# A two-layer decoder trunk in split fp32: matmul widths in runs of four, wide projections for the short convolution, the decays' clamp on ACT

## The chip, the cores and the metric

The kernel runs on one core of a Trainium2 chip. A core has five engines with a queue each: PE (TensorE, the matmuls; PEld is its loading of the stationary operand), DVE (VectorE), ACT (ScalarE), POOL (GpSimd) and SP (SyncE, which here issues loads). Each works its queue in order and waits at an instruction until what that one needs is there. Matmuls write PSUM, which has eight banks of 128 x 512 fp32 numbers; the other data is in SBUF, and weights come from HBM by DMA.

The metric is the device time of one execution in microseconds (us). Three runs of the kernel before gave 1529.78 (median), 1529.49 and 1533.1 us.

## The reference

256 tokens of width 1024 pass two layers. In each: a SwiGLU FFN (width 2816), a mixer, a second FFN, and a gated embedding; every step is normed first and added to the stream `h`.

```python
def swiglu(x, wg, wu, wd):
    return (jax.nn.silu(x @ wg) * (x @ wu)) @ wd

def hybrid_mixer(u, w_in, ...):
    proj = u @ w_in
    sc_b, sc_c, sc_x, m_z, m_xbc, m_dt, gate_a, gate_m = jnp.split(proj, PROJ_SPLITS, axis=-1)
    y_a = (sc_b * causal_depthwise_conv(sc_c * sc_x, sc_conv_w)) @ sc_w_out
    xbc = jax.nn.silu(causal_depthwise_conv(m_xbc, m_conv_w) + m_conv_b)
    xs, bm, cm = jnp.split(xbc, ...)
    ...
    y = ssd_chunked(xh * dt[..., None], A * dt, bm, cm)
    ...
    merged = jax.nn.sigmoid(gate_a) * y_a + jax.nn.sigmoid(gate_m) * y_m
    return merged @ w_o
```

In `ssd_chunked` the sequence is cut into two chunks of 128 tokens. Inside a chunk the weight of token s for token l is `exp(a_cum[l] - a_cum[s])` for s <= l and zero otherwise, times a product of the group's `C` and `B`; there are 32 heads in 4 groups of 8.

## The kernel before

**Split products.** Every matmul operand is held as two numbers: `hi`, a rounded copy, and `lo`, the rest. A product is hi x hi + hi x lo + lo x hi. Weights come as raw fp32 by SP's DMAs (`fetch`, 512 KB each); `half` lets ACT write `whi` (L98) and DVE `wlo` (L96). A chunk of weights is two such halves of four k-blocks each (k runs over the 1024 inputs in eight blocks of 128). Up to five raw and seven split halves are alive (`NRAW`, `NHALF`); a new split starts when TensorE has used an old one up.

**Two forms of a projection.** Both have 128 weight columns standing and the 256 tokens moving, with the tokens' hi and lo parts side by side in `both` (512 columns). `ws` (L213) issues three matmuls of 256 columns for each k: `wh` with hi, `wh` with lo, `wl` with hi, all into one half of a bank; two calls (`ws2`) make a chunk of 256 output columns, 48 matmuls, one bank. `wide_ws` (L232) issues two for each k: `wh` with all 512 columns of `both`, so that hi and lo results land in the two halves of a bank, and `wl` with 256 columns into the first half. A bank takes 16 matmuls; what is in its halves has to be added afterwards. Gate and up products in the FFN use it (`up`, L402, two banks a step, 18 steps in each of four FFNs) and `both_parts` (L387) joins the halves with an ACT copy and a DVE add. The mixer's projections use `ws2`.

**The mixer.** `ORDER` lists the large steps of a layer: `bc` and `xs` (projections with the long convolution), `sc` (the short convolution's three projections for each of four groups: g.0 gives `xsb`, g.1 is multiplied with it and convolved in `sc_conv`, g.2 gates it in `sc_gate`), `z`, `ga`, `gm`, `so`. `LAGS` puts the small steps of each SSD group so many large steps behind it. `turn` transposes `xsil` (a convolved `xs`) on TensorE, and ACT copies it to `xg`; `weigh` makes `xw` from `xg` on DVE, and `states` multiplies it on TensorE. `decay` (L960) loads the rows of `a_cum` into `m` by a DMA on ACT's queue, subtracts each token's own `acum` and clamps at 0 on DVE (L968, eight heads one by one), takes `Exp` on ACT and multiplies with the group's `cbm`. `outputs` queues the products of `m` and `xd`, and `drip` slips them in between the matmuls of a later projection. The order within each engine's queue is then set by the framework's scheduler.

**The code around the change.**

Of the kernel before, what the change touches and what calls it, by code (L numbers as in the profile page):

```python
# [8 lines left out]
F32 = mybir.dt.float32  # L9
F32R = mybir.dt.float32r  # L10
BF16 = mybir.dt.bfloat16
AF = mybir.ActivationFunctionType
ALU = mybir.AluOpType
# [3 lines left out]
P = 128  # L17
# [5 lines left out]
KD = D // P  # L23
# [12 lines left out]
NT2 = 8  # L36
# [23 lines left out]
def trunk(ctx: ExitStack, tc: tile.TileContext, a: dict, out: bass.AP):  # L60
    nc = tc.nc
# [10 lines left out]
    def nm(s):  # L72
        cnt[0] += 1
        return f"{s}_{cnt[0]}"

    def bank():
        return psp.tile([P, 512], F32, tag="ps", name=nm("ps"))

    def mm(o, l, r, start, stop):
        return nc.tensor.matmul(o, lhsT=l, rhs=r, start=start, stop=stop).ins  # L80
# [55 lines left out]
    def chunk(name, i, c, kn):  # L136

        key = (name, i, c)
        sources[key] = (a[name][i, c], kn)
        return key  # L140
# [52 lines left out]
    def xpair():  # L193

        both = act.tile([P, KD, 2, NT, P], F32R, tag="xx", name=nm("xx"), bufs=2)
        return both[:, :, 0], both[:, :, 1], both.rearrange("p k s t c -> p k (s t c)")
# [11 lines left out]
    def drip(n=1):  # L208
        for _ in range(min(n, len(fill))):
            fill.pop(0)()  # L210


    def ws(o, wc, cols, x, t=None):  # L213
        xh, xl, _ = x
        for k in range(KD):
            wh, wl = wc[k]
            rh = xh[:, k] if t is None else xh[:, k, t]
            rl = xl[:, k] if t is None else xl[:, k, t]
            mm(o, wh[:, cols], rh, k == 0, False)
            mm(o, wh[:, cols], rl, False, False)  # L220
            mm(o, wl[:, cols], rh, False, k == KD - 1)
            drip()

    def ws2(ps, wc, x, t=None):

        for b in range(2):
            o = ps[:, b * 256:(b + 1) * 256] if t is None else ps[:, b * 256 + t * P:b * 256 + (t + 1) * P]
            ws(o, wc, slice(b * P, (b + 1) * P), x, t)

    def wide_ws(o, wc, cols, x):  # L232
        xh, _, both = x
        for k in range(KD):
            wh, wl = wc[k]
            if k < KD - 1:
                mm(o, wh[:, cols], both[:, k], k == 0, False)
                mm(o[:, 0:256], wl[:, cols], xh[:, k], False, False)
            else:
                mm(o[:, 0:256], wl[:, cols], xh[:, k], False, False)  # L240
                mm(o, wh[:, cols], both[:, k], False, True)


    def as_(os, lh, ll, rh, rl, first, last):
# [135 lines left out]
    class FFN:  # L380
        def __init__(self, i, gu, dn, gname, ple=None):
# [20 lines left out]
            def up(j):  # L402
                def f(wc):
                    banks[j] = [bank(), bank()]
                    for b in range(2):
                        wide_ws(banks[j][b], wc, slice(b * P, (b + 1) * P), prep.x)
                    evac(j)
                return f, [chunk(gu, i, j, KD)]
# [187 lines left out]
    class Mixer:  # L596
        def __init__(self, i):
# [3 lines left out]
            S = self  # L601
# [6 lines left out]
            def step(fn, *keys):  # L608
                add_.append((fn, keys))
# [38 lines left out]

            def sc_step(g, n):
                def f(wc):  # L650
                    ps = bank()
                    ws2(ps, wc, S.prep.x)
                    if n == 0:
                        if g == 0:
                            S.sct = xpair()
                        S.xsb[g] = mp.tile([P, 512], F32, tag="t2", name=nm("xsb"), bufs=NT2)
                        nc.scalar.activation(S.xsb[g], ps, AF.Copy)
                    elif n == 1:
                        S.sc_conv(g, ps)
                    else:  # L660
                        S.sc_gate(g, ps)
                step(f, chunk("w_sc", i, g * 3 + n, KD))

            def z_run(g, kh, ts):
# [175 lines left out]
        def t2(self, what, shape=(P, GW)):  # L840
            return self.pool.tile(list(shape), F32, tag="t2", name=nm(what), bufs=NT2)

        def conv_silu(self, ps, blk, dst):

            ac = self.t2("ac", (P, 2, 256))
            for b in range(2):
                q = blk + b
                src = ps[:, b * 256:(b + 1) * 256]
                nc.scalar.activation(ac[:, b], src, AF.Identity, scale=self.convw[:, q, 3:4], bias=self.convb[:, q:q + 1])  # L849
                for s in range(1, 4):  # L850
                    nc.vector.scalar_tensor_tensor(ac[:, b, s:256], src[:, 0:256 - s], self.convw[:, q, 3 - s:4 - s],  # L851
                                                   ac[:, b, s:256], op0=ALU.mult, op1=ALU.add)
            nc.scalar.activation(dst, ac, AF.Silu)
# [106 lines left out]
        def decay(self, g, c):  # L960
            mp = self.pool
            cbm = mp.tile([P, P], F32, tag="cbm", name=nm("cbm"), bufs=2)
            nc.vector.tensor_tensor(cbm, self.cps[g][:, c * P:(c + 1) * P], upper, op=ALU.mult)
            self.ms[g, c] = m = mp.tile([P, HG, P], F32, tag="m", name=nm("m"), bufs=2)
            r0 = c * HEADS + g * HG
            nc.scalar.dma_start(m, self.acD[r0:r0 + HG, :].rearrange("(o h) l -> o h l", o=1).partition_broadcast(P))
            for hh in range(HG):
                nc.vector.tensor_scalar(m[:, hh], m[:, hh], self.acum[:, r0 + hh:r0 + hh + 1], 0.0, op0=ALU.subtract, op1=ALU.min)  # L968
            nc.scalar.activation(m, m, AF.Exp)
            nc.vector.tensor_tensor(m, m, cbm.unsqueeze(1).broadcast_to([P, HG, P]), op=ALU.mult)  # L970

        def weigh(self, g):
# [180 lines left out]
```

## Time and profile before

| | |
|---|---|
| runs | 1529.49, 1529.78, 1533.1 us |
| profiled execution, its time | 1528.8 us |
| its span, first to last instruction | 1527.0 us |
| mean granted TensorE clock | 0.999 |
| FFN 1 of layer 0, gate and up products, then down | from 16 to 188 us of the span |
| mixer of layer 0 | about 205 to 541 us |
| FFN 2 of layer 0, then the embedding | 556 to 758 us |
| layer 1, the same three | from 774, 960 and 1311 us |

The page lists each engine's busy time, its share in 40 slices of the span, the chain of work that ended last, and groups of like instructions. A group's row reads: line, engine, operation, what it writes <- what it reads, sizes, count | busy us, mean ns of one | idle time of the engine just before, and what ended it. In a timeline row the first two numbers are the start in us from the span's start and the time taken; TensorE's matmuls overlap their neighbours, so that their cost in a stream is the distance from one start to the next.

### The profile page before, as it was taken

The page shows a single profiled execution, that of the slowest core. Times are in us where ns is not written, and L with a number is a line of the kernel's source. Part 1 is how long each engine was busy: PE and PEld are TensorE (multiplying, and loading weights), DVE is VectorE, ACT ScalarE, POOL GpSimd, SP SyncE. Part 2 cuts the span into 40 slices and gives each one's busy share as a digit, 9 for nine tenths or more (in the row PEclk, how much of TensorE's full clock was granted, in tenths as well). Part 3 has the DMA queues.
Part 4 walks back from the last instruction along what each step waited for, and adds up shares of the span by engine and source line. Part 5 has one row for each costly group of instructions (what it writes and reads, how often), then busy time and mean ns, then how long its engine had stood idle before and what let it go on. Part 6 is the DMA issues. An engine that isn't in the chain of part 4 may idle for free.

```text
span 1527.0 us, 22369 instructions
## 1 busy us (share of the span) xinstructions
PE 1512.6 (99%) x8561; PEld 1313.0 (86%) x8561; DVE 1039.5 (68%) x1543; ACT 880.6 (58%) x1254; POOL 24.7 (2%) x41
## 2 busy tenths in 40 slices
PE   9999999999999999999999999999999999999998
PEld 6888889999988878888878888899999888888886
DVE  6666468898865577664677655688979655766545
ACT  6665366667564366653656654675666544666544
POOL 0000000000000000000000000000000000000000
PEclk9999999999999999999999999999999999999999
DMA  7655566555546555556565555665555555655542
GB/s 275 207 193 183 176 207 198 187 184 180 185 155 197 192 196 191 182 191 193 170 216 180 182 191 167 205 205 186 191 178 176 166 192 182 217 187 186 189 157 90
DMA packets 85437, 285.68 MB, mean 187 GB/s; under 512 B 10577, under 2 KB 10961, under 8 KB 85330
## 3 DMA queue, kind: packets, MB, share of 16 engines
q1 hardware_dynamic: 77968, 267.94, 53.9%
q10 hardware_dynamic: 7362, 16.31, 3.1%
q8 instruction: 67, 1.10, 0.3%
q14 instruction: 40, 0.33, 0.1%
HBM read 283.10 MB, written 1.11 MB: 186 GB/s over the span
## 4 chain that ended last, share of the span: by engine, by line
PE 94%; DVE 3%; issue 1%; ACT 1%; POOL 0%; POOLq 0%; ACTq 0%; DVEq 0%
PE ps L80 92%; DVE wlo L96 2%; PE ps L273 1%; DVE xn L329 1%; PE ps L636 0%; POOL rstd L289 0%; ACT junk L321 0%; DVE xx L277 0%; PE ps L435 0%; ACT whi L98 0%; DVE h L534 0%; DVE h L1030 0%; DVE sg L589 0%; DVE var L283 0%; DVE h L590 0%
## 5 line engine op out<-in xcount | busy, mean ns | idle before, releaser
L96 DVE TENSOR_TENSOR wlo<-raw,whi 128x1024 fp32r<-128x1024 f32 x508 | 616.6, 1223 | 356.3 <-ACT whi L98 345.6
L98 ACT ACTIVATE whi<-raw 128x1024 fp32r<-128x1024 f32 x508 | 534.2, 1058 | 332.9 <-PE ps L80 302.6
L80 PE MATMUL ps<-xx,whi 128*128 128x256 f32 (+1 forms) x2688 | 685.8, 336 | 0.0
L80 PE MATMUL ps<-xx,wlo 128*128 128x256 f32 x1920 | 517.1, 282 | 0.0
L80 PEld LDWEIGHTS ps<-xx,whi 128*128 128x128 f32 x2688 | 446.9, 190 | 44.6 <-issue 4.3
L80 PEld LDWEIGHTS ps<-xx,wlo 128*128 128x128 f32 x1920 | 364.7, 190 | 13.4
L80 PE MATMUL ps<-whi,xx 128*128 128x512 f32 (+1 forms) x1168 | 367.7, 392 | 2.3 <-ACT whi L98 1.4
L80 PEld LDWEIGHTS ps<-whi,xx 128*128 128x128 f32 x1168 | 218.0, 188 | 47.7 <-ACT whi L98 2.7
L80 PE MATMUL ps<-wlo,xx 128*128 128x512 f32 (+1 forms) x584 | 222.8, 388 | 0.6 <-DVE wlo L96 0.6
L80 PE MATMUL ps<-whi,hh 128*128 128x512 f32 x352 | 137.3, 390 | 0.0
L80 PE MATMUL ps<-wlo,hh 128*128 128x512 f32 x352 | 136.9, 389 | 0.0
L80 PEld LDWEIGHTS ps<-wlo,xx 128*128 128x128 f32 x584 | 109.9, 188 | 23.1 <-DVE wlo L96 2.2
L80 PE MATMUL ps<-whi,hl 128*128 128x512 f32 x352 | 113.6, 389 | 0.0
L80 PEld LDWEIGHTS ps<-whi,hl 128*128 128x128 f32 x352 | 66.1, 188 | 13.8
L80 PEld LDWEIGHTS ps<-wlo,hh 128*128 128x128 f32 x352 | 66.1, 188 | 13.6
L80 PEld LDWEIGHTS ps<-whi,hh 128*128 128x128 f32 x352 | 66.1, 188 | 13.4
L851 DVE SCALAR_TENSOR_TENSOR ac<-ps,convw,ac 128x255 f32<-128x255 f32 (+1 forms) x144 | 67.9, 477 | 9.5 <-ACT ac L849 8.1
L389 ACT ACTIVATE sg<-ps 128x256 f32<-128x256 f32 x72 | 27.7, 384 | 64.5 <-PE ps L80 64.5
L80 PE MATMUL ps<-whi,yh 128*128 128x512 f32 x128 | 50.0, 390 | 0.0
L80 PE MATMUL ps<-wlo,yh 128*128 128x512 f32 x128 | 49.8, 389 | 0.0
L396 ACT ACTIVATE sg<-sg 128x256 f32<-128x256 f32 x72 | 30.0, 417 | 33.3 <-DVE sg L390 33.3
L389 ACT ACTIVATE pr<-ps 128x256 f32<-128x256 f32 x72 | 27.7, 385 | 36.9 <-PE ps L80 36.9
(153 smaller groups left out, 1087.8 us busy)
## 6 DMA issues: line engine op xcount, KB each, us to landing
raw<-in_gu SPq DMA_DIRECT2D x176, 512.0 KB, 3.8
raw<-in_dn SPq DMA_DIRECT2D x88, 512.0 KB, 3.6
raw<-in_w_xbc SPq DMA_DIRECT2D x48, 512.0 KB, 4.1
raw<-in_w_sc SPq DMA_DIRECT2D x48, 512.0 KB, 4.1
raw<-in_w_z SPq DMA_DIRECT2D x32, 512.0 KB, 3.9
raw<-in_w_mo SPq DMA_DIRECT2D x32, 512.0 KB, 3.9
raw<-in_w_ga SPq DMA_DIRECT2D x16, 512.0 KB, 4.3
m<-acD ACTq DMA_DIRECT2D x16, 512.0 KB, 4.9
```

What stands on the lines that cost most here:

```text
L80: return nc.tensor.matmul(o, lhsT=l, rhs=r, start=start, stop=stop).ins
L96: return nc.vector.tensor_tensor(lo, src, hi.bitcast(F32), op=ALU.subtract).ins
L98: up = nc.scalar.activation(hi, src, AF.Copy).ins
L273: nc.tensor.transpose(tp[:, j * P:(j + 1) * P], src[:, c:c + P], ident)
L329: ins = nc.vector.scalar_tensor_tensor(xn[:, sl], h[t][:, sl], r, g, op0=ALU.mult, op1=ALU.mult)
L389: nc.scalar.activation(v, ps[:, 256:512], AF.Copy)
L396: nc.scalar.activation(gate, gate, AF.Silu)
L851: nc.vector.scalar_tensor_tensor(ac[:, b, s:256], src[:, 0:256 - s], self.convw[:, q, 3 - s:4 - s], ac[:, b, s:256], op0=ALU.mult, op1=ALU ...
```

## The change

There are three edits. `wide_ws` follows a list, `FOURS`, of (k, part) pairs: two wide matmuls, four narrow, four wide, four narrow, two wide; with the next bank's first two that makes runs of four. It now drips as well. The short convolution's steps call a new `wide`, which takes two banks, joins their halves into one tile `v` of the pool `t2` (eight buffers), and hands `v` to `sc_conv` and `sc_gate` in place of the PSUM bank. In `decay` ACT takes `Relu(acum - m)`, head by head, with a pointer bias, in place of DVE's subtract and min, and `Exp` gets scale -1.

```diff
+    FOURS = [(k, s) for s, ks in enumerate((range(2), range(4), range(2, 6), range(4, 8), range(6, 8))) for k in ks for s in (s % 2,)]
+
     def wide_ws(o, wc, cols, x):
         xh, _, both = x
-        for k in range(KD):
-            wh, wl = wc[k]
-            if k < KD - 1:
-                mm(o, wh[:, cols], both[:, k], k == 0, False)
-                mm(o[:, 0:256], wl[:, cols], xh[:, k], False, False)
+        for n, (k, s) in enumerate(FOURS):
+            if n == KD + 2:
+                drip(KD // 2)
+            if s == 0:
+                mm(o, wc[k][0][:, cols], both[:, k], k == 0, k == KD - 1)
             else:
-                mm(o[:, 0:256], wl[:, cols], xh[:, k], False, False)
-                mm(o, wh[:, cols], both[:, k], False, True)
+                mm(o[:, 0:256], wc[k][1][:, cols], xh[:, k], False, False)
+        drip(KD // 2)
...
             def sc_step(g, n):
                 def f(wc):
-                    ps = bank()
-                    ws2(ps, wc, S.prep.x)
+                    v = S.wide(wc, "xsb" if n == 0 else "scv")
                     if n == 0:
                         if g == 0:
                             S.sct = xpair()
-                        S.xsb[g] = mp.tile([P, 512], F32, tag="t2", name=nm("xsb"), bufs=NT2)
-                        nc.scalar.activation(S.xsb[g], ps, AF.Copy)
+                        S.xsb[g] = v
                     elif n == 1:
-                        S.sc_conv(g, ps)
+                        S.sc_conv(g, v)
                     else:
-                        S.sc_gate(g, ps)
+                        S.sc_gate(g, v)
...
+        def wide(self, wc, what):
+
+            pss = [bank(), bank()]
+            for b in range(2):
+                wide_ws(pss[b], wc, slice(b * P, (b + 1) * P), self.prep.x)
+            v = self.t2(what)
+            for b in range(2):
+                o = v[:, b * 256:(b + 1) * 256]
+                nc.scalar.activation(o, pss[b][:, 256:512], AF.Copy)
+                nc.vector.tensor_tensor(o, o, pss[b][:, 0:256], op=ALU.add)
+            return v
...
             for hh in range(HG):
-                nc.vector.tensor_scalar(m[:, hh], m[:, hh], self.acum[:, r0 + hh:r0 + hh + 1], 0.0, op0=ALU.subtract, op1=ALU.min)
-            nc.scalar.activation(m, m, AF.Exp)
+                nc.scalar.activation(m[:, hh], m[:, hh], AF.Relu, scale=-1.0, bias=self.acum[:, r0 + hh:r0 + hh + 1])
+            nc.scalar.activation(m, m, AF.Exp, scale=-1.0)
```

Instructions in the queues: the orders of SP and POOL stay as they were; ACT and DVE have the same order as before in the FFNs and another one in the mixers. ACT's table loads go from 47 to 51.

On TensorE, the first gate bank of the first FFN (`ps_83_374`; `whi_59_302` and `whi_62_308` are the hi parts of its weights' two halves, `wlo_60_303` and `wlo_63_309` the lo parts, `xx` the tokens). Before:

```order
L80 MATMUL ps_83_374<-xx_7_112,whi_59_302 128x512
L80 MATMUL ps_83_374<-xx_7_112,wlo_60_303 128x256
L80 MATMUL ps_83_374<-xx_7_112,whi_59_302 128x512
L80 MATMUL ps_83_374<-xx_7_112,wlo_60_303 128x256
L80 MATMUL ps_83_374<-xx_7_112,whi_59_302 128x512
L80 MATMUL ps_83_374<-xx_7_112,wlo_60_303 128x256
L80 MATMUL ps_83_374<-xx_7_112,whi_59_302 128x512
L80 MATMUL ps_83_374<-xx_7_112,wlo_60_303 128x256
```

After the change, the whole bank:

```order
L80 MATMUL ps_83_374<-xx_7_112,whi_59_302 128x512 x2
L80 MATMUL ps_83_374<-xx_7_112,wlo_60_303 128x256 x4
L80 MATMUL ps_83_374<-xx_7_112,whi_59_302 128x512 x2
L80 MATMUL ps_83_374<-xx_7_112,whi_62_308 128x512 x2
L80 MATMUL ps_83_374<-xx_7_112,wlo_63_309 128x256 x4
L80 MATMUL ps_83_374<-xx_7_112,whi_62_308 128x512 x2
```

The matmuls are the same sixteen; their order is now two wide, four narrow, four wide, four narrow, two wide, and the last use of each half of the weights is where it was.

On ACT, the first mixer, where SSD group 0's `xsil` is transposed and copied to `xg` (`m_530` and `m_541` before, `m_536` and `m_549` after, are the group's decays of chunk 0 and 1; `xsb` and `sca` belong to the short convolution's group 1). Before:

```order
L969 ACTIVATE m_541_2797<-m_541_2797 128x1024
L853 ACT_TABLE_LOAD
L853 ACTIVATE xsil_511_2614<-ac_512_2615 128x512
L657 ACTIVATE xsb_520_2686<-ps_519_2637 128x512
L98 ACTIVATE whi_534_2779<-raw_533_2777 128x1024
L98 ACTIVATE whi_537_2785<-raw_536_2783 128x1024
L637 ACTIVATE xg_471_2320<-ps_539_2789 128x2x256
L862 ACTIVATE sca_532_2770<-xsb_520_2686,scw_402_1901 128x256 x2
L637 ACTIVATE xg_471_2320<-ps_542_2809 128x2x256
```

After:

```order
L984 ACTIVATE m_536_2664<-m_536_2664 128x1024
L867 ACT_TABLE_LOAD
L867 ACTIVATE xsil_516_2582<-ac_517_2583 128x512
L853 ACTIVATE xsb_526_2639<-ps_524_2605 128x256
L853 ACTIVATE xsb_526_2639<-ps_525_2606 128x256
L853 ACTIVATE scv_539_2710<-ps_537_2676 128x256
L853 ACTIVATE scv_539_2710<-ps_538_2677 128x256
L98 ACTIVATE whi_542_2725<-raw_541_2723 128x1024
L98 ACTIVATE whi_545_2731<-raw_544_2729 128x1024
L876 ACTIVATE sca_540_2716<-xsb_526_2639,scw_402_1901 128x256 x2
L641 ACTIVATE xg_472_2308<-ps_547_2735 128x2x256
L983 ACTIVATE m_549_2743<-m_549_2743,acum_494_2399 128x128 x8
```

The second copy to `xg` and then the `Exp` of `m_549` follow these rows. Four copies out of PSUM stand where one did, and chunk 1's eight relus have come between the two copies to `xg`; the `Exp` of chunk 1, which stood ahead of `xsil`, now stands behind them. In the second layer the order at this place is the same.

## The prediction

> **What bounds the kernel now.** I read the page's parts 1, 2 and 4 first: who is busy, at what clock, and which engine the last-ending chain runs through.
>
> ```profile
> PE 1512.6 (99%) x8561; PEld 1313.0 (86%) x8561; DVE 1039.5 (68%) x1543; ACT 880.6 (58%) x1254; POOL 24.7 (2%) x41
> PEclk9999999999999999999999999999999999999999
> PE 94%; DVE 3%; issue 1%; ACT 1%; POOL 0%; POOLq 0%; ACTq 0%; DVEq 0%
> L98 ACT ACTIVATE whi<-raw 128x1024 fp32r<-128x1024 f32 x508 | 534.2, 1058 | 332.9 <-PE ps L80 302.6 <-issue 16.6 <-DMA raw<-in_gu 6.8
> ```
>
> TensorE is busy in every slice at the full granted clock, and 94% of the chain runs through it. The last row says who waits for whom: ACT, which prepares the weights, sits idle 302.6 us until TensorE hands a weight buffer back, and only 6.8 us for a load. So weights come ahead of need, and time is won only by shortening what stands in TensorE's own queue; it is lost when a product has to wait for an operand. Next, busy time by engine in the stretch of gate and up products and in the mixer's dense stretch:
>
> ```profile
> core 0: us, PE busy (x) PEld busy (x) DVE busy (x) ACT busy (x) POOL busy (x), PEclk, DMA share, GB/s
> 41.35:131.50 90.15, 90.15 (x514) 78.37 (x513) 62.43 (x100) 56.88 (x99) 0.00 (x0) 1.00 0.58 191
> 229.00:397.00 168.00, 168.00 (x1296) 160.80 (x1295) 144.33 (x272) 110.60 (x147) 2.85 (x4) 1.00 0.56 186
> ```
>
> In both TensorE has no gap. In the first DVE and ACT are 69% and 63% busy; in the second DVE is 86% busy and ACT 66%.
>
> **Widths in runs, gate and up.** The start-to-start time of matmuls is what a chain of them costs. Two rows of the chain view (start, length, matmuls) give it for long runs of one width, 48 of 256 columns and 252 of 512:
>
> ```profile
> 271.10 5.75 PE ps L80 x48
> 464.06 57.16 PE ps L80 x252
> ```
>
> That is 0.1198 and 0.2268 us each. The timeline (start, time, tile, count) shows one gate or up bank of 16 matmuls, today alternating, from one bank's last wide matmul to the next bank's:
>
> ```profile
> 60.70 0.63 PE L80 MATMUL ps<-xx,whi 128*128 128x512 f32 x2
> 61.17 0.28 PE L80 MATMUL ps<-xx,wlo 128*128 128x256 f32 x1
> ...
> 63.28 0.40 PE L80 MATMUL ps<-xx,wlo 128*128 128x256 f32 x2
> 63.52 0.63 PE L80 MATMUL ps<-xx,whi 128*128 128x512 f32 x2
> ```
>
> A bank takes 63.52 - 60.70 = 2.82 us. At the long-run pitches its eight wide and eight narrow matmuls would take 8 x 0.2268 + 8 x 0.1198 = 2.773, so the fourteen changes of width cost 0.047 together. The change keeps four of them. What a run of only four costs is read where widths change once; first wide to narrow, then narrow to wide:
>
> ```profile
> 34.91 0.28 PE L80 MATMUL ps<-xx,wlo 128*128 128x256 f32 x1
> 35.02 0.40 PE L80 MATMUL ps<-xx,whi 128*128 128x512 f32 x1
> ...
> 359.27 0.40 PE L80 MATMUL ps<-whi,xx 128*128 128x512 f32 x1
> 359.50 0.40 PE L80 MATMUL ps<-wlo,xx 128*128 128x512 f32 x1
> 359.74 0.62 PE L80 MATMUL ps<-whi,xx 128*128 128x512 f32 x2
> 360.20 0.39 PE L80 MATMUL ps<-wlo,xx 128*128 128x512 f32 x1
> ```
>
> The first narrow one after a wide run takes 0.11, and the first four wide ones after a narrow run 360.20 - 359.27 = 0.93 instead of 0.907: a wide run pays some settling. Four narrow are 0.11 + 3 x 0.12 = 0.47, four wide 0.93; two of each make 2.80. There are 18 steps x 2 banks x 4 FFNs = 144 banks, so I take 144 x 0.02 = **2.9 us saved**. The best case is no settling, 144 x 0.047 = 6.8. The worst is the two wide matmuls at 60.70, 61.17 - 60.70 = 0.47 or 0.235 each, for all wide ones: 8 x 0.235 + 8 x 0.12 = 2.84, 2.9 us lost. I take the settling rows because they are the nearest to runs of four. TensorE is gapless there, so all of it counts.
>
> [...]
>
> **The short convolution's projections.** There are 24 chunks (12 a layer). Each goes from 48 narrow matmuls, 5.75 us by the row above, to two banks of the new form, 2 x 2.80 = 5.60: 24 x 0.15 = **3.6 us saved** (5.55 and 4.9 at best, 5.68 and 1.7 at worst). TensorE's stretch 229 to 397 is gapless too, so this counts in full. The small products that are dripped between the matmuls come in fours instead of singly; they are as many as before, and I cost that at nothing.
>
> What comes in for it, with the price of each:
>
> ```profile
> L389 ACT ACTIVATE pr<-ps 128x256 f32<-128x256 f32 x72 | 27.7, 385 | 36.9 <-PE ps L80 36.9
> L390 DVE TENSOR_TENSOR sg<-sg,ps 128x256 f32<-128x256 f32 x72 | 30.4, 422 | 17.8 <-ACT sg L389 17.8
> L968 DVE TENSOR_SCALAR m<-m,acum 128x128 f32<-128x128 f32 x128 | 28.8, 281 | 0.0
> L862 ACT ACTIVATE sca<-xsb,scw 128x256 f32<-128x256 f32 x16 | 7.2, 498 | 0.9 <-DVE xsb L857 0.9
> L98 ACT ACTIVATE hh<-pr 128x256 fp32r<-128x256 f32 x72 | 30.2, 419 | 14.7 <-DVE pr L397 14.7
> L853 ACT ACT_TABLE_LOAD x12 | 15.4, 1283 | 0.2
> m<-acD ACTq DMA_DIRECT2D x16, 512.0 KB, 4.9
> ```
>
> A chunk's two halves are joined by two copies on ACT (0.385 each) and two adds on DVE (0.422): 9.2 and 10.1 us a layer. The decays' 64 clamps a layer leave DVE (64 x 0.281 = 18 us). So DVE, the busier of the two, gets lighter.
>
> **The clamp as relu.** No row has 128x128 on ACT with a pointer bias. From 1024 to 256 columns ACT goes from 1.058 to 0.419 us, 0.83 ns a column, so L862 (256 columns, one pointer) less 128 columns is 0.39 us; the bounds are 0.31 (the 419 row less 128 columns, no pointer) and 0.50 (L862 whole). Two of L862 in a row take 0.90 (row at 278.21 below), so each that follows another costs 0.1 less: eight relus take 0.39 + 7 x 0.30 = 2.5 us, and 64 a layer some 20. With two more table loads (2.6) and the copies ACT gains about 30 us a layer, in a stretch where it now is idle 34%. The weights' splits hide that. The DMA that brings `m` was waited for by DVE, and is now waited for by ACT; 4.9 us pass from issue to landing, and behind the first relu stand a table load, `bc`, `xx` and weight splits. Weights are far ahead; I cost that wait at nothing. SP's and POOL's orders stay as they are; the eight DMAs of `m` a layer stay on ACT's queue.
>
> [...]
>
> One place where ACT has the later work is group 0's `xw`. Rows of the timeline now:
>
> ```profile
> 274.81 0.63 ACT L853 ACTIVATE xsil<-ac 128x512 f32<-128x512 f32 x1
> 275.35 0.58 ACT L657 ACTIVATE xsb<-ps 128x512 f32<-128x512 f32 x1
> 275.83 2.01 ACT L98 ACTIVATE whi<-raw 128x1024 fp32r<-128x1024 f32 x2
> 276.69 1.04 PE L636 MATMUL ps<-ident,xsil 128*128 128x128 f32 x8
> 278.21 0.90 ACT L862 ACTIVATE sca<-xsb,scw 128x256 f32<-128x256 f32 x2
> 279.01 0.58 ACT L637 ACTIVATE xg<-ps 128x512 f32<-128x512 f32 x1
> 281.47 0.69 DVE L974 TENSOR_TENSOR xw<-xg,w 128x512 f32<-128x512 f32 x1
> 283.31 1.02 PE L80 MATMUL ps<-xw,btok 128*128 128x512 f32 x2
> ```
>
> `xw` ends at 282.16, 1.15 before TensorE takes it. In the new order ACT does, from the end of `xsil` at 275.44: four copies (4 x 0.29), two splits (2.0), `sca` (0.9), `xg` (0.5), eight relus (2.5) and the second `xg` (0.57), in sum 7.6, so `xg` is there at 283.1 and `xw` at 283.8. What stands ahead of `xsil` comes out even: eight relus (2.5) more, one `Exp` and one table load (2.3) less. TensorE, with five shorter chunks behind it and one more ahead (0.15 each), wants `xw` 0.7 to 0.9 earlier than now, about 282.5. That is **1.3 us of waiting**, in each of two layers: 2.6 us. The bounds are 0 (relus of 0.31) and 2.4 a layer (relus of 0.50, pitch 0.40 or more). After that wait every later operand has that much more time, so I add none further on.
>
> **Sum.** 2.9 + 3.6 - 2.6 = 3.9 us off the profiled execution's 1528.8 gives 1524.9. The median of the runs, 1529.78, lies 1.0 above it, so I name **1525.9 us**. A measurement of this kernel tells about 0.3%, 4.6 us, from no change; the forecast, by itself 1523.3 to 1528.5, lies mostly within that.
>
> **Rivals.** One: the runs settle less and ACT keeps up. Long-run pitches give 6.8 + 4.9 = 11.7, 1518.1; my own gains with no wait give 1523.3. For it: the constant 0.2268 over 252 matmuls; against it the settling rows. Two: the order of widths is worth nothing. A bank stays at 2.82, a chunk becomes 5.64, 24 x 0.11 = 2.6, and the wait takes it back: 1529.8. For it: the wide pair at 0.235 each in today's stream. Three, slower: ACT becomes the late engine in the mixer. The relus stand ahead of both `xsil` and the second `xg`; with waits for `m` in the queue (up to 4.9 where too little stands between its DMA and its relu), TensorE waits there. From 3.3 us a layer the gain of 6.5 is gone, from 5.5 it is slower by over 0.3%; with 6 a layer it is 1535. For it: margins of about a microsecond where ACT gets 30 us more; against: ACT's 34% of idle time and DVE's relief. That the matmuls might not come in fours is no rival: the order shows them so.
>
> **Chances.** Forecast 0.40 (0.12 of it below 1525.2, beyond 0.3%), rival one 0.30, two 0.18, three 0.12. So faster 0.12 + 0.30 = 0.42, same 0.28 + 0.18 = 0.46, slower 0.12. The range takes in rival one to its end and the unknown costs but for all at their worst at once (2.9 lost, 1.7 gained, 4.8 waited: 1535.8), which lies with rival three: 1518 to 1533.5, and leaves out little more than 0.1.
>
> **What would show it.** A gate or up bank of 2.80 us (2.77: rival one; 2.82: two), a projection chunk of 5.60 instead of 5.75; relus near 0.39; TensorE idle before `xw` of group 0 by about 1.3 us with DVE's `xw` as the releaser, and nowhere else in the mixer. Idle time before `xsil`'s transposes, or several microseconds before `xw`, would mean that I costed ACT too low.

## The result, and the profile after

Four runs of the changed kernel gave 1542.45 to 1544.51 us, median 1544.12; the runs of the kernel before beside them had a median of 1531.44. The ratio is 1.0083, with an interval of 1.0070 to 1.0096: **slower by 0.8%**, above the predicted range, where a gain was forecast. The times of the kernel before lie on two levels, about 1529.5 and 1533.3, and the traces show a like step ahead of everything that was changed (the first FFN's long run of products starts at 41 to 42 us in ten of the profiled executions, at 45 in five), while two single runs far above, of 3883 and 2411 us in the first experiment, are in no ratio. The profiled execution has a span of 1540.3 us, 13.3 more than before, and a mean granted clock of 0.995.

The page's busy times and its chain by engine and by line, after the change:

```profile
PE 1513.8 (98%) x8177; PEld 1295.2 (84%) x8177; DVE 1030.1 (67%) x1463; ACT 933.6 (61%) x1426; POOL 24.3 (2%) x41
PE 88%; DVE 5%; ACT 3%; issue 2%; DMA 1%; POOL 0%; POOLq 0%; ACTq 0%; DVEq 0%
```

TensorE's products should take some 6 us less (6.5 by the prediction) and yet it is busy 1.2 us longer, which already says that some ran slowly; its share of the chain went from 94% to 88%. What took its place is in the view of waits of TensorE (what waits, for whom, us in total, times, longest); these three of its rows are new:

```profile
PE ps L640 <- ACT xsil L867: 7.4, 4, 3.7
PE ps L80 <- DVE xw L989: 3.2, 2, 1.6
...
PE ps L277 <- DVE y L1036: 1.1, 2, 0.5
```

Where the time sits in the program, from the chain view: the start of the first mixer's projections and the long run of 252 matmuls near its end, first for the kernel before (whose run of 252 the prediction quotes), then for the changed one, whose FFN stretch stands in front:

```profile
41.35 147.58 PE ps L80 x772
204.85 23.97 PE ps L80 x136
```

```profile
41.70 147.14 PE ps L80 x772
204.74 23.98 PE ps L80 x136
471.10 57.16 PE ps L80 x252
```

The FFN's gate and up piece got 0.44 us shorter. The mixer took 464.06 + 57.16 - 204.85 = 316.37 us and now takes 471.10 + 57.16 - 204.74 = 323.52: 7.15 more, in the second layer 6.95. The place is ACT's queue before the transposes of group 1's `xsil`. ACT and TensorE there after the change, from the timeline (start, time, engine, line; in brackets the idle time before it and what ended it):

```profile
292.02 0.55 ACT L863 ACTIVATE ac<-ps,convb,convw 128x256 f32<-128x256 f32 x1
296.58 0.33 ACTq L980 DMA_DIRECT2D m<-acD  x1
296.96 0.57 ACT L863 ACTIVATE ac<-ps,convb,convw 128x256 f32<-128x256 f32 x1 [4.39 <-PE ps L80]
297.96 1.06 ACT L98 ACTIVATE whi<-raw 128x1024 fp32r<-128x1024 f32 x1 [0.43 <-PE ps L80]
299.40 1.06 ACT L98 ACTIVATE whi<-raw 128x1024 fp32r<-128x1024 f32 x1 [0.38 <-PE ps L80]
300.99 1.28 ACT L983 ACTIVATE m<-m,acum 128x128 f32<-128x128 f32 x4 [0.54 <-DMA m<-acD]
302.29 1.28 ACT L867 ACT_TABLE_LOAD   x1
303.58 0.63 ACT L867 ACTIVATE xsil<-ac 128x512 f32<-128x512 f32 x1
```

```profile
299.82 1.39 PE L80 MATMUL ps<-xd,m 128*128 128x64 f32 x11
304.26 1.12 PE L640 MATMUL ps<-ident,xsil 128*128 128x128 f32 x4 [3.05 <-ACT xsil L867]
```

Read it from the top. The load of the next `m` stands in ACT's queue between the two `ac`, and its issue waits until TensorE has used up an older `m` (there are two buffers). The second `ac` waits behind it, 4.39 us; at most the last 1.5 of these are the issue's doing, since DVE works on the first `ac` until 295.46. Four relus of that new `m` stand ahead of `xsil` and wait for the landing at 300.97. Then come a table load and `xsil`, while TensorE has been idle since 301.21. In the chain it reads as one string, the load from 296.58 to 300.97 and then ACT's own work. The first three rows are group 0's: the load of its first block, from which the chain runs through ACT's queue to `xsil`, and the eight relus of its second block ahead of its `xg`, behind which TensorE waited for `xw`:

```profile
255.68 5.56 DMA m<-acD
...
275.70 0.63 ACT xsil L867
...
280.59 2.33 ACT m L983 x8
...
296.58 4.38 DMA m<-acD
...
301.30 0.97 ACT m L983 x3
...
302.29 1.28 ACT L867
...
303.58 0.64 ACT xsil L867
```

The wait has a second price. The view of windows (stretch, its length, busy time of each engine, then the granted clock) around the wait for `xw`, behind the wait for `xsil`, and behind that of the second layer:

```profile
282.60:284.30 1.70, 0.06 (x2) 0.06 (x1) 0.89 (x3) 1.68 (x4) 0.00 (x0) 1.00 0.27 72
302.65:309.47 6.82, 5.21 (x17) 4.53 (x18) 6.19 (x14) 5.71 (x14) 0.55 (x1) 0.50 0.51 163
309.47:314.00 4.53, 4.53 (x21) 3.74 (x21) 1.40 (x3) 1.93 (x2) 0.00 (x0) 1.00 0.01 3
1067.23:1070.65 3.42, 3.42 (x13) 3.05 (x13) 3.14 (x7) 2.88 (x10) 0.00 (x0) 0.50 0.17 40
```

TensorE worked 5.21 and 3.42 us at half clock. There the 512-column products began 0.427 us apart (six, from 306.67 to 309.23 us), behind it 0.226 (fifteen, from 310.05 to 313.44). From these I put the cost at half of each stretch: 2.6 and 1.7. Before, the clock reads 0.50 only from 1524 us on, when TensorE has no more products.

### The profile page after: what moved, and what is told of

The parts are those of the page before. It is cut to its first block, busy times and chain, and to the rows that moved or that the text cites. A ratio compares the mean times of both kernels' runs of the same rounds, so it can differ in the third digit from the quotient of the medians.

```text
span 1540.3 us, 21647 instructions
## 1 busy us (share of the span) xinstructions
PE 1513.8 (98%) x8177; PEld 1295.2 (84%) x8177; DVE 1030.1 (67%) x1463; ACT 933.6 (61%) x1426; POOL 24.3 (2%) x41
## 4 chain that ended last, share of the span: by engine, by line
PE 88%; DVE 5%; ACT 3%; issue 2%; DMA 1%; POOL 0%; POOLq 0%; ACTq 0%; DVEq 0%
PE ps L80 86%; DVE wlo L96 2%; PE ps L277 1%; DMA m<-acD 1%; ACT whi L98 1%; ACT m L983 1%; DVE xn L333 1%; PE ps L640 0%; ACT L867 0%; POOL rstd L293 0%; DVE xx L281 0%; ACT xsil L867 0%; ACT junk L325 0%; PE ps L439 0%; DVE h L538 0%
## 5 line engine op out<-in xcount | busy, mean ns | idle before, releaser
L80 PE MATMUL ps<-xx,whi 128*128 128x512 f32 (+1 forms) x2304 | 571.6, 361 | 0.0
L80 PEld LDWEIGHTS ps<-xx,whi 128*128 128x128 f32 x2304 | 381.1, 190 | 38.1 <-issue 4.3
L80 PE MATMUL ps<-xx,wlo 128*128 128x256 f32 x1920 | 353.0, 281 | 0.0
L80 PEld LDWEIGHTS ps<-xx,wlo 128*128 128x128 f32 x1920 | 309.0, 189 | 32.4
L293 POOL TENSOR_TENSOR rstd<-var,mhalf 128x1 f32<-128x1 f32 x34 | 23.4, 691 | 1511.1 <-DVE var L287 999.5
```

Of the source, the lines that this page charges most:

```text
L293: nc.gpsimd.tensor_tensor(r, v, mhalf, op=ALU.pow)
```

## The experiments

**The parts, one by one.** First theory: the relus are late on ACT. Rivals: the joins of the wide short convolution are, or the new order of widths costs TensorE itself something.

The clamp back on DVE, the rest as changed:

```diff
-                nc.scalar.activation(m[:, hh], m[:, hh], AF.Relu, scale=-1.0, bias=self.acum[:, r0 + hh:r0 + hh + 1])
-            nc.scalar.activation(m, m, AF.Exp, scale=-1.0)
+                nc.vector.tensor_scalar(m[:, hh], m[:, hh], self.acum[:, r0 + hh:r0 + hh + 1], 0.0, op0=ALU.subtract, op1=ALU.min)
+            nc.scalar.activation(m, m, AF.Exp)
```

> The changed kernel with its clamp back on DVE (subtract and min, Exp with scale 1); runs of four and the wide short convolution stay. Theory (the relus on ACT, behind the DMA of m, are late for TensorE): the four waits of TensorE for xsil and xw (3.05 and 1.64 us in layer 0, 3.72 and 1.54 in layer 1) are gone, the granted clock stays at 1.0 in the mixers, and of the changes only the shorter banks are left: 144 x 0.0133 = 1.9 us and 24 chunks x about 0.15 = 3.6 us less than the kernel before, so 1525 to 1527 us. Rival one (the joins of the wide short convolution, with their copies on ACT and two PSUM banks, are what is late): the waits stay, 1538 us or more. Rival two (the order of widths with its dripped fours costs TensorE itself time): no waits, but 1531 us or more.

1532.26 us median, ratio 1.0 (0.9989 to 1.0011). The waits for `xsil` and the half clock are gone, so the relus are needed for the loss. But the predicted gains did not come out either. Its new waits, and in the chain view its first 282 matmuls of the mixer's dense stretch beside the 346 of before:

```profile
PE ps L277 <- DVE y L1036: 2.3, 2, 1.2
PE ps L80 <- DVE xw L989: 1.7, 2, 0.8
```

```profile
228.80 41.23 PE ps L80 x282
```

```profile
229.09 41.90 PE ps L80 x346
```

The chunks are shorter, by 0.67 us for four of them or 0.17 each (predicted 0.15), about 2.0 us a layer. DVE then hands over `xw` of a later group and `y` too late, which takes 2.0 us a layer back.

The reverse edit on the kernel before, relus alone:

> The kernel before with nothing but the clamp as relu on ACT. The scheduler here puts the relus at places of its own: eight of group 1's chunk 0 behind the xsil of its first half and ahead of that of its second, three of group 0's chunk 1 ahead of xsil and five ahead of the second xg. Theory: slower than before, since relus and the DMA of m stand ahead of operands that TensorE wants within a microsecond: waits for xw or xsil of 1 to 4 us in each layer, 2 to 10 us in all, with a lower granted clock only behind a wait of 3 us or more. Rival one (the wide short convolution alone is at fault): no wait of TensorE in the mixers over 0.6 us, time within 1 us of before.

1531.09 us, ratio 1.0003 (0.9992 to 1.0013). A miss for the theory as I had put it: relus on ACT alone cost nothing that can be measured. Here the scheduler put group 1's relus behind the first `xsil`.

Runs of four alone, in the kernel before:

> The kernel before with nothing but the gate and up banks in runs of four. Theory: a bank goes from 2.822 to 2.809 us, 144 banks, 1.9 us less; nothing changes in the mixers and no wait appears. Rival two (the order of widths or its drips costs time): the same or slower than before, a bank at 2.82 us or more.

1529.11 us, ratio 0.9984 (0.9974 to 0.9995): faster, by the 1.9 us expected within the interval. The piece of 772 matmuls takes 147.15 us instead of 147.58.

```profile
45.10 147.15 PE ps L80 x772
```

The wide projections alone, the clamp on DVE as in the first of these kernels and the widths alternating:

```diff
-    FOURS = [(k, s) for s, ks in enumerate((range(2), range(4), range(2, 6), range(4, 8), range(6, 8))) for k in ks for s in (s % 2,)]
+    FOURS = [p for k in range(KD - 1) for p in ((k, 0), (k, 1))] + [(KD - 1, 1), (KD - 1, 0)]
```

> The kernel before with nothing but the short convolution's projections in the 512-column form, wide and narrow matmuls alternating as they did in gate and up, clamp on DVE. Theory: 24 chunks of 5.64 in place of 5.75 us, 2.6 us less than before, and 2.6 us more than the kernel that has runs of four too (144 x 0.0133 + 48 x 0.0133); no wait of TensorE over 0.6 us in the mixers. Rival one (the joins are late): waits for xsil or xw of 1 us or more, time at or above that of before.

1531.7 us, ratio 1.0007 (0.9997 to 1.0017): no gain, where 2.6 us were expected, with waits of 0.80 us for `xw` and of 1.03 us ahead of `y`'s transposes in each layer. So rival one is right in part. So the loss of 13 us belongs to none of the parts. It appears where relus and wide projections meet, in one order of ACT's queue.

**What in ACT's queue.** The next four kernels are to tell the amount of the work there from its place. One of the eight decay blocks of a layer (group 1, chunk 0), whose relus stood ahead of `xsil`, back on DVE:

```diff
-            for hh in range(HG):
-                nc.scalar.activation(m[:, hh], m[:, hh], AF.Relu, scale=-1.0, bias=self.acum[:, r0 + hh:r0 + hh + 1])
-            nc.scalar.activation(m, m, AF.Exp, scale=-1.0)
+            if (g, c) != (1, 0):
+                for hh in range(HG):
+                    nc.scalar.activation(m[:, hh], m[:, hh], AF.Relu, scale=-1.0, bias=self.acum[:, r0 + hh:r0 + hh + 1])
+            else:
+                for hh in range(HG):
+                    nc.vector.tensor_scalar(m[:, hh], m[:, hh], self.acum[:, r0 + hh:r0 + hh + 1], 0.0, op0=ALU.subtract, op1=ALU.min)
+            nc.scalar.activation(m, m, AF.Exp, scale=-1.0 if (g, c) != (1, 0) else 1.0)
```

> The changed kernel, but for one of the eight decay blocks of each layer (group 1, chunk 0) the clamp is on DVE again; the other seven stay relus on ACT. The runs so far showed that neither the relus alone nor the wide short convolution alone cost more than 1 us, so the loss comes where both meet. Theory: it is this one place, where the DMA of m and four relus of the block stand ahead of group 1's xsil. Then the two waits for xsil (3.05 and 3.72 us) and TensorE's half clock behind them (3.4 and 1.7 us) go, 11.9 us in all, and the time is 1531 to 1534 us, with group 0's waits for xw (1.6 each) still there. Rival (the loss is the sum of all relus' work on ACT, an eighth of which goes here): 1541 us or more.

1555.09 us, ratio 1.0153 (1.0125 to 1.0180). Both expectations failed: slower still. ACT in that run:

```profile
302.99 0.33 ACTq L980 DMA_DIRECT2D m<-acD  x1
303.41 1.28 ACT L867 ACT_TABLE_LOAD   x1 [1.20 <-PE ps L80]
304.70 0.63 ACT L867 ACTIVATE xsil<-ac 128x512 f32<-128x512 f32 x1
305.24 0.55 ACT L863 ACTIVATE ac<-ps,convb,convw 128x256 f32<-128x256 f32 x1
310.27 0.99 ACT L984 ACTIVATE m<-m,acum 128x128 f32<-128x128 f32 x3 [4.49 <-DMA m<-acD]
```

With four relus fewer the scheduler drew the load of the **next** `m` ahead of `xsil`. Its issue waits for TensorE's last product with an older `m`, and then the next block's relus stand ahead of `xg` and the second `xsil` and wait 4.49 us for the landing. TensorE waits 15.5 us for `xsil` in all, up to 4.34 at once. The place makes the loss, and the place moves with every edit.

The loads of `m` from POOL's queue instead of ACT's:

```diff
-            nc.scalar.dma_start(m, self.acD[r0:r0 + HG, :].rearrange("(o h) l -> o h l", o=1).partition_broadcast(P))
+            nc.gpsimd.dma_start(m, self.acD[r0:r0 + HG, :].rearrange("(o h) l -> o h l", o=1).partition_broadcast(P))
```

> The changed kernel with the DMAs of m issued from POOL's queue instead of ACT's, so that ACT no longer stands in its queue until TensorE gives back a buffer of m; it still waits for the landing at its first relu. Two relus now stand ahead of group 1's xsil in the first half, none of the second ac. Theory A (the issue that waits for the buffer is what makes ACT late): the waits for xsil are under 0.6 us and the time is 1533 us or less. Theory B (the landing is what ACT waits for, wherever the issue stands): the buffer is free at 296.2, the data there at about 301, xsil at 302.5 to 303, 1.5 to 2.5 us of waiting in each layer, 1534 to 1541 us.

1544.21 us, ratio 1.0089 (1.0075 to 1.0104). Theory A falls: as slow as without the edit, with waits of 6.05 and 5.01 us for group 1's `xsil`. The landing is what ACT waits for, as B has it, and later than B said, since the load lands 7.5 us after its issue. The second `ac`, with no issue ahead of it, comes no earlier, for DVE now works longer on the first one:

```profile
295.97 0.54 POOL L980 DMA_DIRECT2D m<-acD  x1 [40.52 <-DVE ac L865]
297.25 0.57 ACT L863 ACTIVATE ac<-ps,convb,convw 128x256 f32<-128x256 f32 x1 [3.69 <-DVE ac L865]
...
303.47 0.69 ACT L983 ACTIVATE m<-m,acum 128x128 f32<-128x128 f32 x2 [3.76 <-DMA m<-acD]
304.18 1.28 ACT L867 ACT_TABLE_LOAD   x1
305.47 0.63 ACT L867 ACTIVATE xsil<-ac 128x512 f32<-128x512 f32 x1
```

No load at all:

```diff
-            nc.scalar.dma_start(m, self.acD[r0:r0 + HG, :].rearrange("(o h) l -> o h l", o=1).partition_broadcast(P))
-                nc.scalar.activation(m[:, hh], m[:, hh], AF.Relu, scale=-1.0, bias=self.acum[:, r0 + hh:r0 + hh + 1])
+                nc.scalar.activation(m[:, hh], upper, AF.Relu, scale=-1.0, bias=self.acum[:, r0 + hh:r0 + hh + 1])
```

> The changed kernel without the DMAs of m: the relus read the resident 128x128 mask in place of the loaded rows of a_cum, so that this kernel leaves out the load and computes other decays; every relu, Exp and buffer of m stays. The scheduler puts all eight relus of group 1's chunk 0 ahead of its xsil, where the changed kernel has four. Theory (ACT waits for the load of m, 4.4 us of it): with eight relus but no load there the wait for xsil is under 0.6 us in both layers, the clock stays up, and the time is 1525 to 1532 us. Rival (the relus' own time ahead of xsil is the cost): eight cost 1.2 us more than four, the wait for xsil is 3 to 5 us in each layer, 1540 us or more.

1535.7 us, ratio 1.0034 (1.0022 to 1.0046). Between the two: the waits for `xw` are gone, and the wait for `xsil` is 2.17 us a layer with eight relus ahead of it, where it was 3.05 and 3.72 with four relus and a load. By time the load is the larger part, 8.4 us between the medians, though the order of the queue changed with it. The relus' own time and the wait for a buffer, now in front of the first relu (3.82 us), remain, and the wait for `y` is 1.25 us a layer.

Relus for groups 2 and 3 only; the same edit with another condition:

```diff
+            if g >= 2:
```

> The changed kernel with the relus on ACT for groups 2 and 3 alone, the clamp on DVE for groups 0 and 1. With all clamps on DVE the run showed TensorE waiting for DVE's xw of group 2 (0.8 us a layer) and y (1.2 us a layer), which ate the shorter projections. Theory: in the second half of the mixer DVE is the late engine and the relus there relieve it; the waits for xsil and xw of groups 0 and 1 do not come back, those for xw of group 2 and y shrink, and the span lies 2 to 5 us under that of before. Rival (those waits come from the joins' place in DVE's queue and not from its load): waits as with all clamps on DVE, the same time as before within 1 us.

1526.36 us, ratio 0.9981 (0.9970 to 0.9992): **faster than both kernels**. Its whole list of new waits is one row:

```profile
PE ps L277 <- DVE y L1040: 1.1, 2, 0.5
```

```profile
208.19 24.03 PE ps L80 x136
466.29 57.16 PE ps L80 x252
```

The wait for `xw` is gone and that for `y` is half of that with all clamps on DVE; the mixer takes 466.29 + 57.16 - 208.19 = 315.26 us, 1.1 less than before. So in the second half of the mixer the relus do relieve DVE.

**Place or amount.** All eight blocks on ACT, but the relus of three (group 0 chunk 1, both of group 1) made to follow `xg`: a small DVE operation first writes their bias as `xg` times 0 plus `acum`, and group 0's second `decay` is called later. The DVE operation:

```diff
+            late = sm.tile([P, HG], F32, tag="late", name=nm("late"), bufs=2)
+            nc.vector.scalar_tensor_tensor(late, self.xg[g][:, c, 0:HG], 0.0, bias, op0=ALU.mult, op1=ALU.add)
```

> The changed kernel with all eight decay blocks of a layer as relus on ACT, but the relus of three blocks (group 0 chunk 1, both of group 1) made to follow the second copy to their group's xg: their bias is a copy of acum that one small DVE operation of 128x8 makes from xg times 0 plus acum, and group 0's second decay is called behind its second turn. The amount of work on ACT is as in the changed kernel; only its place is another. The DMAs of m stay on ACT's queue, where now both of group 1 stand ahead of the first xsil (the first ahead of the second ac, the second directly ahead of xsil). Theory (two things in ACT's queue are late: the relus that wait for the load, and the issue of the load that waits for a buffer of m): the waits for xw of group 0 (1.6 us) go; at group 1's first xsil about 2.4 us of waiting stay, from the issue of the second DMA, which waits for TensorE's last product of group 0, and the table load and xsil behind it; with the half clock 1529 to 1534 us. Rival (the amount of relu work on ACT decides): 1540 us or more.

> The same kernel with the DMAs of m on POOL's queue, so that neither relus nor issues of m stand ahead of group 1's xsil on ACT, with as many relus on ACT as in the changed kernel. Theory: no wait of TensorE for xsil or xw over 0.6 us, the granted clock at 1.0 through both mixers, and the gains that were predicted for the shorter banks and chunks left over: 1523 to 1528 us. With the DMAs on POOL alone the run gave 1544 us, and with the relus behind alone it should give about 1531. Rival (the amount decides): as slow as the changed kernel.

1549.09 us (ratio 1.0113, 1.0095 to 1.0130) and 1541.12 us (1.0057, 1.0043 to 1.0071). Neither fits, and one reason is not in ACT's queue: a part of the matmuls had become slower. In the second run:

```profile
466.13 58.36 PE ps L80 x252
```

58.36 / 252 is 0.2316 us instead of 0.2268. What these two kernels had added in memory was the tile `late`, 64 bytes a partition. So both were made again with `acum` written over itself, and that tile's size was tried alone in the kernel before.

```diff
+                nc.vector.scalar_tensor_tensor(bias, self.xg[g][:, c, 0:HG], 0.0, bias, op0=ALU.mult, op1=ALU.add)
```

> The kernel with the relus made to follow xg was disturbed: its added tile of 64 bytes a partition went with a pitch of 0.2316 us in the down products in place of 0.2268, some 12 us over the whole kernel. Here the same order is made without a new tile: the small DVE operation writes acum over itself (xg times 0 plus acum). DMAs of m on ACT's queue. Theory: pitch again 0.2268; no wait for xw of group 0 over 0.8 us; about 2.4 us at group 1's first xsil from the issue that waits for the second buffer of m; with the half clock 1529 to 1534 us. Rival (the amount of relu work on ACT decides): 1540 us or more.

1540.36 us, ratio 1.0058 (1.0043 to 1.0073): slower than the theory's 1529 to 1534. The two waits at group 1's `xsil` are as foretold, 2.42 us from the issue of a load directly ahead of it, and the wait ahead of the product of `xw` fell to 0.74 and 0.72 (the view names the small DVE operation behind `xw`). But TensorE now waits 1.41 us for group 0's `xsil` in the first layer, which I had not seen coming. The chain leads from there back to the first load of `m`, which took 6.94 us to land, against 5.56 in the changed kernel:

```profile
255.77 6.94 DMA m<-acD
```

A part of the loss, 1 us or more in each mixer, I cannot place.

> The same without a new tile, with the DMAs of m on POOL's queue: neither relus nor issues of m ahead of group 1's xsil, all eight blocks as relus on ACT. In the disturbed run waits of 1.24 us stayed at group 1's xsil, with no half clock in either layer. Theory: pitch 0.2268, waits for xsil of 1.3 us or less, clock at 1.0, 1524 to 1530 us. Rival (the amount decides): 1538 us or more.

1531.71 us, ratio 1.0013 (1.0001 to 1.0024): slower than the theory's 1524 to 1530, and the clock did fall once (last section), but far from the rival's 1538. With as many relus on ACT as in the changed kernel, the loss against the kernel before is 1.4 us in place of 12.7 (medians), once neither relus nor loads stand ahead of `xsil`. What is left of the wait for group 1's `xsil`, 1.24 us a layer, is the table load:

```profile
299.91 1.28 ACT L867 ACT_TABLE_LOAD   x1
301.21 0.63 ACT L867 ACTIVATE xsil<-ac 128x512 f32<-128x512 f32 x1
```

So with only the loads moved the kernel took 1544.2 us, with only the relus moved 1540.4, with both 1531.7. The amount is not free: the last is 5 us above the kernel with half of the relus. And the tile alone, in the kernel before:

```diff
+    pad = [sm.tile([P, 8], F32, tag="pad", name=f"pad{n}", bufs=2) for n in range(2)]
+    for t in pad:
+        nc.vector.memset(t, 0.0)
```

> The kernel before with nothing but an unused tile of 128x8 fp32 in two buffers (64 bytes a partition) in the pool of small tiles, which moves what is allocated behind it. Theory: the slower matmuls of the two disturbed runs come from the moved addresses: down products at 0.2316 us in place of 0.2268 and a time of about 1540 us. Rival (something else in those runs, the chip or the new order): pitch 0.2268 and the time of before.

1540.67 us, ratio 1.0058 (1.0041 to 1.0075), with the same slow pitch and no new wait:

```profile
469.56 58.36 PE ps L83 x252
```

## Why the prediction was wrong

- **Gate and up banks**: right, and mis-sized a little. The piece of 772 matmuls lost 0.44 us, the like pieces of the four FFNs together 1.7 instead of 2.9. The two-digit starts of single rows were too coarse for a difference of 0.02.
- **The projections**: a chunk is 0.17 us shorter (0.15 predicted). "TensorE's stretch 229 to 397 is gapless too, so this counts in full" failed: alone, the gain is given back by waits for DVE's `xw` and `y`. A gapless stretch shows that no wait is there yet, not how much margin the operands have. Only with relus in the late groups does part of it show.
- **A relu's price**: right, eight take 2.33 us in the chain (2.5 predicted).
- **The wait at group 0's `xw`**: right in place and kind, 1.64 and 1.53 us (1.3 predicted), but the figure is in part luck. "What stands ahead of `xsil` comes out even" left out the landing of the first `m`: `xsil` ended at 276.33 instead of 275.44. From there to the end of the second `xg` ACT took 7.1 us instead of 7.6, which made up for more than half of that.
- **The step that failed**: "The DMA that brings `m` was waited for by DVE, and is now waited for by ACT; ... I cost that wait at nothing", and with it "After that wait every later operand has that much more time, so I add none further on". I looked at ACT's new order at group 0 alone. At group 1 an issue that waits for a buffer, the landing, four relus and a table load come in one string ahead of `xsil`, and TensorE waits 3.05 and 3.72 us: 0.54 and 1.20 for the landing, 1.3 for the relus, and 1.2 for the table load, which before did not stand there and stays where relus and loads were moved away. That weights are far ahead was true and beside the point: what is behind in ACT's queue is not only weights.
- **Not in the sum at all**: the half clock behind that wait, 2.6 and 1.7 us.

The mechanism was my rival three, which I gave 0.12 and 6 us of waiting a layer. In these terms it was about 9 in the first mixer: the 7.15 lost and the 2.0 that shorter chunks saved. This includes the half clock, which that rival did not have either. For one mixer (the first) the account is: waits 1.64 + 3.05 + 0.31 + 0.54 = 5.5, half clock 2.6, shorter chunks -2.0, in sum 6.1 of the measured 7.15. About 1 us a layer I cannot assign. In the changed kernel relus on ACT pay for groups 2 and 3, where DVE has the later work (1526.36 us, against 1532.26 with every clamp on DVE), and lose when groups 0 and 1 have them too, where ACT has it (1544.12 us).

What was shown: the relus and the loads of `m` ahead of `xsil` make nearly all the loss (1544 against 1531.7 us with the same relus and loads elsewhere, 1526.4 with half of the relus), though each of these edits changed the order of the queue in other places too. What was only read from the order: that the scheduler moves the loads and relus ahead whenever its own plan has room there.

## What to carry to other kernels

When an operation moves to another engine, follow what it waits for: its wait, and that of the load it reads, becomes the wait of everything behind it in the queue (here four relus waited for a landing until 300.99 us, and `xsil`, behind them and a table load, started at 303.58), so each operand that the bound engine takes from that queue has to be looked up, not the one place where it seems tight. Read the margin (when it was ready against when it was wanted) and not only whether a gap is there now. Where a scheduler sets the order, compare the order of each variant, since an edit in one place moved loads and relus in another.

## What the runs showed of the hardware

**The clock at TensorE's waits.** In the changed kernel it stayed at 1.0 through and behind the waits of 1.64 and 1.53 us (at `xw`), and fell to 0.50 at those of 3.05 and 3.72 us (at `xsil`). The length alone does not decide it. The kernel without loads waited 2.17 us in both layers, and only the first was followed by half clock:

```profile
302.85:305.02 2.17, 0.00 (x1) 0.00 (x1) 2.17 (x4) 2.14 (x4) 0.00 (x0) 0.91 0.85 251
304.61:308.02 3.41, 3.00 (x12) 2.81 (x13) 3.41 (x8) 3.38 (x5) 0.00 (x0) 0.50 0.66 175
1061.31:1063.48 2.17, 0.00 (x1) 0.00 (x1) 2.17 (x4) 2.14 (x4) 0.00 (x0) 1.00 0.74 242
1063.48:1067.00 3.52, 3.52 (x20) 3.12 (x21) 3.52 (x9) 3.49 (x6) 0.00 (x0) 1.00 0.49 149
```

In the kernel with the relus behind `xg` and the loads on POOL the wait was 1.24 us in both layers, and half clock followed it in the first:

```profile
302.16:305.57 3.41, 3.41 (x14) 3.02 (x13) 3.41 (x8) 1.65 (x6) 0.00 (x0) 0.50 0.86 215
1061.46:1066.00 4.54, 4.54 (x25) 3.93 (x26) 4.54 (x11) 2.41 (x6) 0.36 (x1) 1.00 0.79 286
```

So the 3 us or more that I expected for the relus alone, read from the changed kernel's waits, is no limit here: the clock fell at 2.17 and at 1.24 us too. The half clock lasts 3.41 us in these rows and 3.42 in the second layer of the changed kernel; in its first it lasts 6.82, twice as long.

**64 bytes slowed a part of the matmuls.** An unused tile of 64 bytes a partition made the kernel 0.58% slower (1540.67 us), more than any of the change's gains. In its chain the 252 matmuls late in the mixer take 58.36 us, against 57.16 before, and the 796 of the second FFN in layer 0 take 154.68, against 152.99. No slower are the 156 matmuls that begin at 425.01 us in the kernel before, 120 of them 512-column products of `xx` (32.63 us against 32.70), and the 346 of the mixer's dense stretch (41.89 against 41.90). Of the 252 matmuls 180 are products of `yh` and `yl` and 72 of `xx`, and of the 796 another 252 are the FFN's down products (`hh`, `hl`). So I estimate that the products of `yh` and `yl` carry the whole 1.20 us, 0.007 each, and that the 0.2316 above is a mean; no row shows them apart. No view shows addresses, so that the tile acts by moving what is allocated behind it is inferred and not shown; other sizes were not tried.
